# Two transformer layers on one core: a weight tile's last eighth stored apart, one weight load a head sooner, panels that end in turn, splits in a given order

## The chip, the cores and the metric

The kernel runs on one core of one Trainium2 chip. The metric is the device time of one execution in microseconds (us); less is better. Inside a core five engines work side by side, each on its own list of instructions, strictly in the order of that list: TensorE (PE in the profile, with its weight loads as PEld), VectorE (DVE), ScalarE (ACT), GpSimd (POOL) and SyncE (SP). An instruction whose data aren't there yet holds up all that stands behind it on its engine. SP and POOL also issue the DMA transfers that bring weights from device memory.

## The reference

Two consecutive layers work on 512 latent tokens and 256 context tokens of 1024 features, in float32. Each layer normalises and modulates its input, projects it, attends, projects the heads' outputs back to 1024 features (the output projection), adds that to the residual, and runs a gated feed-forward network (FFN).

```python
# layer 0 (even): latent attention heads and neighbourhood heads side by side
p = h @ even_w_in
o = concat(mla_heads(p...), na_heads(p...))        # 8 + 8 heads
x = x + gate * (o @ even_w_out)                    # output projection, 1024 x 1024
x = x + gate * swiglu(modulate(x), w_gate_up, w_down)
# layer 1 (odd): sliding-window grouped-query attention with sinks, latent tokens only
o = swa(h @ odd_w_in)
x = x + gate * (o @ odd_w_out)
x = x + gate * swiglu(modulate(x), w_gate_up, w_down)
return rms_norm(x) * final_norm

def swiglu(h, w_gate_up, w_down):
    g, u = split(h @ w_gate_up)                    # 2 x 2816 features
    return (silu(g) * u) @ w_down
```

## The kernel before, in words

**Layout and precision.** Features lie on the 128 partitions and tokens along the free axis, so an activation of 1024 features is 8 tiles (KT = 8). Every float32 operand is held as two numbers of a shorter type, a high part and a low part. A product of two such operands is three matmuls: high by high, high by low, low by high. In `mm3` (L312) these are L319, L321 and L322; in the FFN's `product` they are L1437 to L1439; in `three`, which the FFN's first panels use, L741 to L743. A raw weight tile `wr` arrives by DMA from SP; ScalarE makes its high part `wh` with a cast, then VectorE the low part `wl` by a subtraction. `load_w` (L299) does this with L308 and L309, `parts` (L1423) with L1424 and L1425.

**Buffers.** `wr`, `wh` and `wl` have three slots each, of 1024 columns. A slot comes free only when the last reader of its old tile is through, so the fourth weight tile of a stretch can't be cast before the first tile's last matmul. `nb` (two slots of 768 columns) holds masks and such.

**Output projection.** `output` (L1302) goes over the 8 blocks m of 128 output features, for each of two streams of tokens. Block m needs one weight tile of 128 x 1024: 8 pieces of 128 columns, one for each of the 8 tiles k of attention output. Its 24 matmuls accumulate over k in one of TensorE's result banks (names starting with ps). Layer 0's stream has 384 tokens, layer 1's 256. The last tiles of attention output come late, since they need the last heads.

**What sets the order.** The program is written with a scheduler that takes the instructions of each engine from a list of ready ones by its own estimate of when they start. So the order on an engine may differ from the text, but is fixed before the program runs. `behind(instruction, mark)` adds an ordering wait behind an earlier instruction. DMA loads of weights are issued on SP in that same way, each as soon as its slot `wr` is free.

**FFN.** Layer 0 has 384-token halves, layer 1 256-token halves. The first gate and up panels (`first_pairs`, L1513) are plain products: the second half of the tokens panel by panel, then the first half with three panels interleaved, k by k, as the loop at L1531 has it. All later panels come as a `Pair` (L1441) with seven products of sums of operands instead of eight (a Strassen-like scheme): `head` two products, `body` three (s2, s3, s1) and `tail` two (s4 for "22", u2 for "T4"). `weights` makes the sums s1 to s4 of the weights on VectorE and splits each into high and low. A chunk of three or four panels (`CHUNKS`, L28; two in layer 0's last) ends with the products of `w_down`. In layer 0's last chunk `keep_groups` loads all of that chunk's `w_down` columns ahead, and the last `output` of layer 0 uses them. `late_step` puts modulation sums of layer 1 (L273, each 128x1024 on VectorE) into FFN stretches.

## Time and profile before

| | |
|---|---|
| time, median of 3 runs | 1554.52 us (1552.96 to 1556.51) |
| the profiled execution's own time | 1556.14 us |
| its span in the profile | 1554.4 us |
| granted clock of TensorE, mean | 0.995 of full speed |
| TensorE busy | 1524.9 us, 98% of the span |
| VectorE, ScalarE, GpSimd busy | 76%, 49%, 13% |
| DMA traffic | 225.95 MB, mean 145 GB/s |

All readings of the trace are of that one profiled execution, which took 1.6 us more than the median; 1.7 us of it lie outside the span. In timeline rows the first two numbers are the start from the span's begin and the length in us, then engine, line, operation, `out<-in`, the shape, and in brackets the idle time before it with the instruction that ended it. Matmuls overlap, so their spacing is read from start to start. Lines are those of the kernel before; the changed kernel's `mm3` has L342, L344 and L345, its residual add L1300, its `parts` L1461 and L1462.

### The profile page before, as it was taken

Reading aid. Unit: us, or ns where it says so; the run is one execution under the profiler, and the core shown is the slowest. Engines: PE = TensorE matmul, PEld = TensorE weight load, DVE = VectorE, ACT = ScalarE, POOL = GpSimd, SP = SyncE. Lnnn points to the kernel's source line nnn. Section 1 sums busy time; section 2 is a strip of 40 time slices with the busy share of each in tenths; the row PEclk is TensorE's granted clock in tenths of the full one; section 3 lists DMA queues with packets and bytes.
Section 4 is the critical chain, followed back from the end, with each engine's and each line's share of the span. In section 5 each row is a group of like instructions: output and inputs, shape, how many; then the busy total and the mean of one; then the engine's idle time right before and its main releaser. Section 6 shows DMA issues by size and latency. Waiting matters only on the chain.

```text
span 1554.4 us, 26610 instructions
## 1 busy us (share of the span) xinstructions
PE 1524.9 (98%) x10032; PEld 1373.6 (88%) x10032; DVE 1182.5 (76%) x2420; ACT 760.7 (49%) x1523; POOL 195.4 (13%) x266
## 2 busy tenths in 40 slices
PE   9999899999999999999999999999999999999998
PEld 8788787878999898999989998877889899898997
DVE  4799987776867686867768667789867779678685
ACT  4533676673555242433424335557846455354453
POOL 0022211000111102012021122560011000000001
PEclk9999999999999999999999999999999999999999
DMA  9675654244643636547375493200224224324322
GB/s 322 245 223 182 161 143 102 57 132 135 216 136 120 232 102 219 174 146 286 117 258 183 165 341 128 68 28 1 96 81 138 82 72 137 105 76 135 89 90 88
DMA packets 80931, 225.95 MB, mean 145 GB/s; under 512 B 11233, under 2 KB 18401, under 8 KB 80801
## 3 DMA queue, kind: packets, MB, share of 16 engines
q1 hardware_dynamic: 61968, 148.73, 30.3%
q0 software_dynamic: 17680, 73.94, 13.8%
q8 instruction: 79, 1.29, 0.3%
q10 hardware_dynamic: 1152, 1.57, 0.3%
q14 instruction: 52, 0.42, 0.1%
HBM read 186.97 MB, written 23.07 MB: 135 GB/s over the span
## 4 chain that ended last, share of the span: by engine, by line
PE 75%; DVE 8%; ACT 2%; issue 2%; DMA 2%; POOL 0%; DVEq 0%; ACTq 0%; POOLq 0%
PE pss L1439 5%; PE pso L530 5%; PE pss L1438 5%; PE pss L1437 5%; PE psd L319 3%; PE psd L321 3%; PE psd L322 3%; PE pss L319 3%; PE pss L322 3%; PE pss L321 3%; PE pst L1439 3%; PE pst L1437 3%; PE pst L1438 3%; PE pst L319 2%; PE pst L321 2%; PE pst L322 2%
## 5 line engine op out<-in xcount | busy, mean ns | idle before, releaser
L308 ACT CAST wh<-wr 128x1024 fp32r<-128x1024 f32 (+2 forms) x147 | 115.1, 798 | 224.1 <-DMA wr<-in_w_dn_dram 44.6
L309 DVE TENSOR_TENSOR wl<-wr,wh 128x1024 fp32r<-128x1024 f32 (+2 forms) x144 | 130.3, 912 | 87.4 <-ACT wh L308 83.2
L537 ACT ACTIVATE p<-p,sm 128x512 f32<-128x512 f32 (+3 forms) x144 | 105.1, 731 | 30.7 <-DVE sm L541 30.1
L1437 PE MATMUL pss<-b,wh 128*128 128x384 f32 (+1 forms) x346 | 107.6, 312 | 0.5 <-ACT b L345 0.5
L1438 PE MATMUL pss<-b,wh 128*128 128x384 f32 (+1 forms) x346 | 107.8, 312 | 0.1
L1439 PE MATMUL pss<-b,wl 128*128 128x384 f32 (+1 forms) x346 | 107.1, 311 | 0.4 <-DVE wl L1425 0.4
L321 PE MATMUL psd<-b,wh 128*128 128x512 f32 (+2 forms) x254 | 88.7, 349 | 0.0
L273 DVE CUSTOM_DVE_ANT_0 p<-rope,cond 128x1024 bf16<-128x1024 f32 x64 | 76.9, 1219 | 12.3 <-DMA rope<-in_mod_w_dram 12.2
L319 PE MATMUL psd<-b,wh 128*128 128x512 f32 (+2 forms) x214 | 78.7, 368 | 0.9 <-ACT wh L308 0.3
L322 PE MATMUL psd<-b,wl 128*128 128x512 f32 (+2 forms) x214 | 77.6, 363 | 0.0
L263 POOL DMA_DIRECT2D rope<-in_mod_w_dram x48 | 25.6, 534 | 411.6 <-DVE mod L273 390.9
L530 PE MATMUL pso<-ph,b 128*64 128x256 f32 (+1 forms) x400 | 77.0, 351 | 0.4 <-DVE ph L475 0.2
L530 PE MATMUL pso<-pl,b 128*64 128x256 f32 (+1 forms) x400 | 77.2, 351 | 0.0
L1439 PE MATMUL pst<-b,wl 128*128 128x384 f32 (+1 forms) x226 | 70.7, 313 | 1.0 <-DVE wl L1425 1.0
L1437 PE MATMUL pst<-b,wh 128*128 128x384 f32 (+1 forms) x226 | 70.6, 313 | 0.6 <-ACT p L1487 0.6
L1438 PE MATMUL pst<-b,wh 128*128 128x384 f32 (+1 forms) x226 | 70.5, 312 | 0.0
L1424 ACT CAST wh<-pl 128x512 fp32r<-128x512 f32 x78 | 45.0, 619 | 51.1 <-PE pss L1438 22.5
L1424 ACT CAST wh<-wr 128x1024 fp32r<-128x1024 f32 x39 | 41.0, 1052 | 56.8 <-PE pst L1438 14.8
L319 PE MATMUL pss<-st,wh 128*128 128x512 f32 (+2 forms) x198 | 67.6, 341 | 0.3 <-ACT wh L308 0.3
L322 PE MATMUL pss<-st,wl 128*128 128x512 f32 (+2 forms) x198 | 67.6, 341 | 0.1
L321 PE MATMUL pss<-b,wh 128*128 128x256 f32 (+2 forms) x208 | 66.0, 317 | 0.0
L1437 PEld LDWEIGHTS pss<-b,wh 128*128 128x128 f32 x346 | 65.0, 188 | 1.1 <-ACT b L345 0.8
(627 smaller groups left out, 5256.8 us busy)
## 6 DMA issues: line engine op xcount, KB each, us to landing
wr<-in_w_gu_dram SPq DMA_DIRECT2D x88, 512.0 KB, 4.0
rope<-in_mod_w_dram POOLq DMA_DIRECT2D x48, 512.0 KB, 3.9
wr<-in_w_dn_dram SPq DMA_DIRECT2D x73, 256.0 KB, 2.8
wr<-in_w_out_dram SPq DMA_DIRECT2D x32, 512.0 KB, 4.0
p<-home POOLq DMA_DIRECT2D x40, 384.0 KB, 5.6
home<-p POOLq DMA_DIRECT2D x40, 384.0 KB, 5.3
wr<-in_w_in_dram SPq DMA_DIRECT2D x21, 512.0 KB, 4.0
ph<-in_mod_w_dram SPq DMA_DIRECT2D x24, 256.0 KB, 3.0
```

The lines of the kernel that those rows point to most:

```text
L273: behind(V.tensor_tensor_reduce(out=T("p", [P, D], mybir.dt.bfloat16), in0=w, in1=cond[:, v, :], op0=ALU.mult, op1=ALU.add, scale=1.0, sca ...
L308: behind(S.copy(h, r), *after[:1])
L309: behind((G if eng else V).tensor_tensor(lo, r, f(h), op=ALU.subtract), *after[1:])
L319: ins = PE.matmul(o, wh[:, k], mh[:, c], start=first and k == 0, stop=False)
L321: PE.matmul(o, wh[:, k], ml[:, c], start=False, stop=False)
L322: PE.matmul(o, wl[:, k], mh[:, c], start=False, stop=last and k == n - 1)
L530: ins = PE.matmul(o[64 * i : 64 * i + 64, c], v(kt), t, start=n == 0, stop=n == len(moving[i]) - 1)
L537: S.activation(p[:, c], p[:, c], AF.Exp, bias=nm, scale=-1.0, accum_out=dn)
L1424: S.copy(h, t)
L1437: PE.matmul(o, wh, xh, start=first and k == 0, stop=False, skip_group_check=not first)
L1438: PE.matmul(o, wh, xl, start=False, stop=False, skip_group_check=not first)
L1439: PE.matmul(o, wl, xh, start=False, stop=k == 3, skip_group_check=not first)
```

## The change

Four things are done.

1. **Ends apart.** For the first three weight tiles of the first stream of both attention output projections, a new `load_ends` takes the place of `load_w`. The raw tile is loaded whole. Its first 896 columns (k = 0 to 6) go to `wh` and `wl` as before, and its last 128 (k = 7) to a piece of a tile `nb`, whose six pieces of 128 columns hold the high and low ends of all three tiles. The class `Ends` picks the right one for k. In layer 0 the first of these tiles is loaded by `mla_jobs` while head 6 of 8 is at work; before, it came after the last head's text.
2. **Panels end in turn.** In layer 1's three interleaved panels, the first four k are interleaved as before, and then each panel's last four k come in one piece, panel after panel.
3. **Splits in order.** In the first pair of each layer 1 chunk, the subtraction that makes s4 and the low part of u2 wait for s2's low part. In layer 0's last pair, and for the first split in `keep_groups`, they wait for the low part of the gate weights.
4. **First products sooner.** At the end of layer 0's FFN, the k = 0 products with the first kept tile (five with its high part) are issued before the last pair's tail; `output` picks up that open bank and goes on from k = 1.

VectorE and ScalarE each have six instructions more, the casts and subtractions of the six ends.

```diff
+    class Ends:
+        def __init__(self, head, end):
+            self.head, self.end, self.n = head, end, head.shape[1] // P
+        def __getitem__(self, at):
+            k = at[1]
+            return self.head[:, k * P : k * P + P] if k < self.n else self.end
+    begun, begun_ends = [], []
+    def load_ends(src, spare, m, after=()):
+        r, n = T("wr", [P, D]), D - P
+        dma(r, src)
+        h, lo = T("wh", [P, n], F32R), T("wl", [P, n], F32R)
+        ends = [spare[:, x * P : x * P + P] for x in (2 * m, 2 * m + 1)]
+        for x, (y, z) in ((r[:, :n], (h, lo)), (r[:, n:], ends)):
+            behind(S.copy(y, x), *after)
+            behind(V.tensor_tensor(z, x, f(y), op=ALU.subtract), *after)
+        return tuple(Ends(x, y) for x, y in zip((h, lo), ends))
...
 # mla_jobs
+            if h == 6:
+                begun_ends.append(T("nb", [P, NT], F32R))
+                begun.append(load_ends(I["w_out0"][0], begun_ends[0], 0))
...
 # output
-                w = kept[m] if keep and i else keep(src, m) if callable(keep) else load_w(src(m), len(mov), P, LOE[l, comp, i], "b" if keep else None, held[m : m + 1] * 2 if i == 0 else ())
+                if comp == 2 and i == 0 and m < 3:
+                    w = begun.pop() if begun else load_ends(src(m), ends(), m, held[m : m + 1])
+                else:
+                    w = kept[m] if keep and i else keep(src, m) if callable(keep) else load_w(src(m), len(mov), P, LOE[l, comp, i], "b" if keep else None)
...
-                o = banks([c], PG)
-                ins = mm3(o, w, mov)
+                n = len(opened)
+                o = opened.pop() if n else banks([c], PG)
+                ins = mm3(o, [x[:, n:] for x in w] if n else w, mov[n:], first=not n)
...
 # Pair.weights
+            self.low = marks["low"]
...
             self.s2 = parts(s2, *(x[:, h[0]] for x in w2))
+            late = {None: (), "g": (self.low,), "s": (marks["low"],)}[self.order]
...
-            V.tensor_tensor(s4, g[:, h[1]], s2, op=ALU.subtract)
+            behind(V.tensor_tensor(s4, g[:, h[1]], s2, op=ALU.subtract), *late)
             self.s4 = parts(s4, *(x[:, h[1]] for x in w3))
-            self.u2 = parts(u[:, h[1]], T("ph", [P, 512], F32R), T("pl", [P, 512], F32R))
+            self.u2 = parts(u[:, h[1]], T("ph", [P, 512], F32R), T("pl", [P, 512], F32R), late)
...
 # first_pairs
-            for x, k in enumerate((0, 4, 1, 5, 2, 6, 3, 7)):
-                for n, o in zip(ns, os):
-                    after = when.pop(len(steps), ())
-                    steps.append(behind(three(o, [y[:, k] for y in ws[n]], ops[a[k // 4]][k % 4], x == 0, x == 7)[0], *after))
+            cut = 4 if l else KT
+            turns = [(x, n, o) for x in range(cut) for n, o in zip(ns, os)]
+            turns += [(x, n, o) for n, o in zip(ns, os) for x in range(cut, KT)]
+            for x, n, o in turns:
+                k, after = (0, 4, 1, 5, 2, 6, 3, 7)[x], when.pop(len(steps), ())
+                steps.append(behind(three(o, [y[:, k] for y in ws[n]], ops[a[k // 4]][k % 4], x == 0, x == 7)[0], *after))
...
 # ffn
-                    p = Pair(l, j, ops, cs, tags[j - k0], (near_done[3],) if j == DIRECT[l] and l == 0 else ())
+                    p = Pair(l, j, ops, cs, tags[j - k0], (near_done[3],) if j == DIRECT[l] and l == 0 else (),
+                             "s" if l and j == k0 else "g" if l == 0 and j == NFF - 1 else None)
...
-            if last:
+            if l == 0 and ci == len(CHUNKS[l]) - 1:
+                o = banks([LATS], PG)
+                first = mm3(o, [x[:, :1] for x in ahead[0]], hs[:1], last=False)
+                opened.append(o)
+                last.tail((first,))
+            elif last:
                 last.tail()
```

How the lists move is seen at three places. The first is TensorE's list at the end of layer 0's attention: `pst` rows are transposes of the last heads' scores (L484 before, L507 after), `pss` rows with 128x384 are the output projection's block 0. Before:

```order
L484 MATMUL pst_4004<-ident_r_90,p_3927 128x128
L484 MATMUL pst_4004<-ident_r_90,p_3958 128x128
L484 MATMUL pst_4011<-ident_r_90,wr_3977 128x128
L484 MATMUL pst_4011<-ident_r_90,p_3987 128x128
L484 MATMUL pst_4011<-ident_r_90,wr_3977 128x128
L484 MATMUL pst_4011<-ident_r_90,p_3987 128x128
L319 MATMUL pss_4252<-b_3502,wh_4248 128x384
L321 MATMUL pss_4252<-b_3503,wh_4248 128x384
L484 MATMUL pst_4032<-ident_r_90,wr_3977 128x128
```

The same place with the change:

```order
L507 MATMUL pst_4013<-ident_r_90,p_3927 128x128
L507 MATMUL pst_4013<-ident_r_90,p_3958 128x128
L342 MATMUL pss_4255<-b_3502,wh_3994 128x384
L344 MATMUL pss_4255<-b_3503,wh_3994 128x384
L345 MATMUL pss_4255<-b_3502,wl_3995 128x384
L342 MATMUL pss_4255<-b_3696,wh_3994 128x384
L344 MATMUL pss_4255<-b_3697,wh_3994 128x384
L345 MATMUL pss_4255<-b_3696,wl_3995 128x384
L342 MATMUL pss_4255<-b_3837,wh_3994 128x384
L344 MATMUL pss_4255<-b_3838,wh_3994 128x384
L345 MATMUL pss_4255<-b_3837,wl_3995 128x384
L507 MATMUL pst_4020<-ident_r_90,wr_3977 128x128
```

Nine products of block 0 now stand ahead of a group of transposes, where two stood behind it.

The second place is TensorE's list where the first three blocks end (`st_4232` and `st_4241` are the high part of attention tile k = 7). Before:

```order
L319 MATMUL pss_4252<-st_4232,wh_4248 128x384
L319 MATMUL psd_4289<-st_4232,wh_4285 128x384
L319 MATMUL pss_4333<-st_4232,wh_4329 128x384
L321 MATMUL pss_4252<-st_4233,wh_4248 128x384
L322 MATMUL pss_4252<-st_4232,wl_4249 128x384
L321 MATMUL psd_4289<-st_4233,wh_4285 128x384
L322 MATMUL psd_4289<-st_4232,wl_4286 128x384
L321 MATMUL pss_4333<-st_4233,wh_4329 128x384
L322 MATMUL pss_4333<-st_4232,wl_4330 128x384
L319 MATMUL pst_4369<-b_3502,wh_4365 128x384
L321 MATMUL pst_4369<-b_3503,wh_4365 128x384
L319 MATMUL pss_4411<-b_3502,wh_4407 128x384
```

With the change:

```order
L345 MATMUL pst_4376<-b_3502,wl_4373 128x384
L342 MATMUL pst_4376<-b_3696,wh_4372 128x384
L344 MATMUL pst_4376<-b_3697,wh_4372 128x384
L345 MATMUL pst_4376<-b_3696,wl_4373 128x384
L342 MATMUL pst_4376<-b_3837,wh_4372 128x384
L342 MATMUL pss_4255<-st_4241,nb_3991 128x384
L342 MATMUL psd_4294<-st_4241,nb_3991 128x384
L342 MATMUL pss_4340<-st_4241,nb_3991 128x384
L344 MATMUL pst_4376<-b_3838,wh_4372 128x384
L344 MATMUL pss_4255<-st_4242,nb_3991 128x384
L345 MATMUL pss_4255<-st_4241,nb_3991 128x384
L344 MATMUL psd_4294<-st_4242,nb_3991 128x384
```

The k = 7 products of blocks 0 to 2 read the ends in `nb`, and products of the next two blocks stand ahead of them.

The third place is VectorE's list in the first pair of a layer 1 chunk. Before (L1467 makes s4; the L1425 row with `pl_13387` is u2's low part, `wl_13365<-ph_13371` is s2's):

```order
L1460 TENSOR_TENSOR ph_13371<-pl_13370,wr_13358 128x512
L1463 TENSOR_TENSOR ph_13376<-wr_13358,wr_13359 128x512
L1274 SCALAR_TENSOR_TENSOR b_12112<-pst_13339,mod_1832_8983,b_12112 128x512
L1467 TENSOR_TENSOR pl_13382<-wr_13358,ph_13371 128x512
L1425 TENSOR_TENSOR pl_13387<-wr_13359,ph_13386 128x512
L1425 TENSOR_TENSOR wl_13365<-ph_13371,wh_13364 128x512
```

With the change:

```order
L1498 TENSOR_TENSOR ph_13385<-pl_13384,wr_13372 128x512
L1502 TENSOR_TENSOR ph_13390<-wr_13372,wr_13373 128x512
L1300 SCALAR_TENSOR_TENSOR b_12119<-pst_13353,mod_1833_8990,b_12119 128x512
L1462 TENSOR_TENSOR wl_13379<-ph_13385,wh_13378 128x512
L1506 TENSOR_TENSOR pl_13396<-wr_13372,ph_13385 128x512
L1462 TENSOR_TENSOR pl_13401<-wr_13373,ph_13400 128x512
```

s2's low part now stands ahead of s4 and of u2's low part. Between the two attention output projections, in layer 1's sliding-window attention, no line of the program is changed, yet the scheduler puts a few of TensorE's instructions there in another order: the two lists differ at 17 places.

More of the change, by code (lines that the diff above doesn't have):

```diff
@@ L1287, in kept_w, with keep_groups @@
         return ahead[m]
-    def keep_groups(k0, kc):
+    def keep_groups(k0, kc, low):
         n = NT // (kc * P)
@@ L1297, in keep_groups @@
                 I["w_dn"][0, a:z, :, k0 * P : (k0 + kc) * P].rearrange("m p c -> p m c"))
-            parts(r[:, c], *(x[:, c] for x in t))
+            parts(r[:, c], *(x[:, c] for x in t), (low,) * (a == 0))
             for m in range(a, z):
@@ L1304, in output, with ends @@
         rest, kept, done = iter(()), [], []
+        spare = []
+        def ends():
+            if not spare:
+                spare.append(begun_ends.pop() if begun_ends else T("nb", [P, NT], F32R))
+            return spare[0]
         for i, (c, v) in enumerate(streams):
@@ L1341, in hybrid_kernel @@
     home = [dr.tile([P, NT], F32, name=f"home{k}") for k in range(KT)]
-    near_done, near_cast = [], []
+    near_done, near_cast, opened = [], [], []
     def combined(src, l, comp, c1, c2):
@@ L1429, in hybrid_kernel, with product @@
     output(lambda m: I["w_out0"][m], O, 0, 2, ((TOK2, 0), (TOK1, 0)), norm, LATE[0])
-    def product(o, w, x, first=False):
+    def product(o, w, x, first=False, after=()):
         for k in range(4):
@@ L1436, in product @@
             xh, xl = x[k]
-            PE.matmul(o, wh, xh, start=first and k == 0, stop=False, skip_group_check=not first)
+            behind(PE.matmul(o, wh, xh, start=first and k == 0, stop=False, skip_group_check=not first), *after)
             PE.matmul(o, wh, xl, start=False, stop=False, skip_group_check=not first)
@@ L1441, in hybrid_kernel, with __init__ @@
     class Pair:
-        def __init__(self, l, j, ops, cs, tag, after=()):
-            self.after = after
+        def __init__(self, l, j, ops, cs, tag, after=(), order=None):
+            self.after, self.order = after, order
             self.l, self.j, self.ops, self.c1, self.c2 = l, j, ops, *cs
@@ L1488, in body, with tail @@
             self.done = marks["middle"] = V.tensor_tensor(self.t[:, self.c2], self.y, self.t[:, self.c2], op=ALU.add)
-        def tail(self):
-            product(self.z, self.s4, self.ops["22"])
+        def tail(self, after=()):
+            product(self.z, self.s4, self.ops["22"], after=after)
             marks["silu"] = S.activation(self.s[:, self.c2], self.z, AF.Silu)
@@ L1557, in ffn @@
                     if l == 0 and j == NFF - 1:
-                        keep_groups(k0, kc)
+                        keep_groups(k0, kc, p.low)
                     p.body()
```

## The prediction

> **What bounds the kernel now.** I read the page's busy rows and chain first, then busy time by stretch, then the engines' timelines at the places where the order moves.
>
> ```profile
> PE 1524.9 (98%) x10032; PEld 1373.6 (88%) x10032; DVE 1182.5 (76%) x2420; ACT 760.7 (49%) x1523; POOL 195.4 (13%) x266
> PE 75%; DVE 8%; ACT 2%; issue 2%; DMA 2%; POOL 0%; DVEq 0%; ACTq 0%; POOLq 0%
> 340.00:384.00 44.00, 40.61 (x260) 32.99 (x257) 27.17 (x52) 21.82 (x42) 0.53 (x1) 1.00 0.45 154
> 1060.00:1140.00 80.00, 78.60 (x641) 62.60 (x639) 71.33 (x237) 63.00 (x152) 0.00 (x0) 1.00 0.14 47
> 1355.00:1362.00 7.00, 6.58 (x57) 6.38 (x56) 7.00 (x12) 3.53 (x8) 0.00 (x0) 1.00 0.45 150
> ```
>
> (The last three rows: stretch, its length, then busy time of PE, PEld, DVE, ACT and POOL, granted clock, DMA share and GB/s.) TensorE bounds the kernel: 98% busy, three quarters of the chain. No matmul is removed here, so the only thing to win is its idle time, 1554.4 - 1524.9 = 29.5 us in all, of which 44.00 - 40.61 = 3.4 us lie in the 44 us where layer 0's attention passes into its output projection. Busy time hides more: matmuls restarting after a wait overlap less, so I count from start to start.
>
> **Ends apart, layer 0.** PE first, then ACT and SP's queue.
>
> ```profile
> 346.71 0.27 PE L484 MATMUL pst<-ident_r,p 128*128 128x128 f32 x1
> 348.22 0.44 PE L319 MATMUL pss<-b,wh 128*128 128x384 f32 x1 [1.24 <-ACT wh L308]
> 349.29 0.27 PE L484 MATMUL psd<-ident_r,wr 128*128 128x128 f32 x1
> 350.07 0.33 PE L484 MATMUL psd<-ident_r,p 128*128 128x128 f32 x1 [0.50 <-ACT p L537]
> 364.78 0.27 PE L484 MATMUL pst<-ident_r,p 128*128 128x128 f32 x1
> 365.40 0.33 PE L484 MATMUL pst<-ident_r,wr 128*128 128x128 f32 x1 [0.35 <-DVE pl L475]
> 374.80 0.34 PE L321 MATMUL pss<-st,wh 128*128 128x384 f32 x1
> 374.98 0.34 PE L322 MATMUL pss<-st,wl 128*128 128x384 f32 x1
> 375.58 0.45 PE L319 MATMUL pst<-b,wh 128*128 128x384 f32 x1 [0.26 <-ACT wh L308]
> 377.48 0.44 PE L319 MATMUL psd<-b,wh 128*128 128x384 f32 x1 [0.34 <-ACT wh L308]
> ...
> 346.21 0.40 ACT L1226 CAST st<-b 128x256 fp32r<-128x256 f32 x1
> 347.12 1.05 ACT L308 CAST wh<-wr 128x1024 fp32r<-128x1024 f32 x1
> 348.06 0.94 ACT L537 ACTIVATE wr<-wr,sm 128x768 f32<-128x768 f32 x1
> 374.48 2.95 ACT L308 CAST wh<-wr 128x1024 fp32r<-128x1024 f32 x3 [2.28 <-PE pss L321]
> ...
> 337.06 3.95 SPq L134 DMA_DIRECT2D b<-in_xn_dram  x8
> ```
>
> A 128x384 product starts 0.18 us after the one before (374.80 to 374.98); a 128x256 product, by its columns, 0.12, a 128x512 product 0.24. The transposes follow each other in about 0.1.
>
> The first tile's cast stands at 347.12, so the first product waits to 348.22: 1.51 - 0.11 = 1.40 us lost. Loaded one head sooner, the tile is cast in an earlier gap (on SP the second tile's load goes out ahead of the eight residual loads of 337.06, which nothing reads before block 0 is summed), and nine products (1.6 us of work) stand where the wait was. The same cast pushed the exponentials (348.06), for which the transpose at 350.07 waits: 0.78 - 0.11 = 0.67. With the cast out of the way I strike that too, and the later one at 365.40, a copy behind a delayed softmax: 0.62 - 0.11 = 0.51. Then the casts of tiles 3 to 5, three in a row from 374.48, start only when the last k = 7 product of tile 0 has let go of a slot. From 374.98 to 377.48 five starts should take 0.88 us and take 2.50: 1.62 lost. With the ends in `nb` the slots are free after k = 6, and other products stand ahead of k = 7. Gone in all: 1.40 + 0.67 + 0.51 + 1.62 = 4.20. Not all stays gone: going through the new lists instruction by instruction with these durations, I find one wait left near 362, where two copies on VectorE stand behind the subtractions of tiles 2 and 3, worth about 0.55. Taken: **3.65**, between 1.0 (only the first wait goes, in part) and 4.2.
>
> The wait is moved onto others: on ScalarE the copies of the scores stand behind the casts of tiles 1 and 2, whose DMAs are issued on SP once a raw slot is free. If a tile lands late, its cast holds those copies, and TensorE waits for them. By the replay tile 2 has about 1 us to spare.
>
> **The split itself.** It adds six casts and six subtractions. The nearest casts are 0.40 for 256 columns and 1.05 for 1024, a line of 0.00085 us a column on a start of 0.18. So 896 + 128 columns cost 0.94 + 0.29, 0.18 more than whole; six tiles 1.1 us of ScalarE, in stretches where ACT is busy 21.82 of 44 us, and as much again on DVE at 27.17. If all lay on the path it would cost 1.1; beside the matmuls nothing. Taken: **-0.3**, as about two of the six fall among the copies TensorE waits for.
>
> [...]
>
> **Ends apart, layer 1.** PE, then ACT:
>
> ```profile
> 1150.10 0.28 PE L322 MATMUL pst<-st,wl 128*128 128x256 f32 x1
> 1151.63 0.39 PE L319 MATMUL psd<-st,wh 128*128 128x256 f32 x1 [0.44 <-ACT wh L308]
> 1152.15 0.38 PE L322 MATMUL pss<-st,wl 128*128 128x256 f32 x1
> ...
> 1149.58 2.94 ACT L308 CAST wh<-wr 128x1024 fp32r<-128x1024 f32 x3 [4.44 <-PE psd L321]
> ```
>
> The three casts begin at 1149.58 after 4.44 us of idle for a product, and TensorE eats them as they come. Five starts from 1150.10 to 1152.15 take 2.05 and should take 0.60: 1.45 lost. By my replay the k = 0 to 6 products of tile 0 end some 2 us before 1149.58, more than the loss. Taken **1.3** (0.6 to 1.45).
>
> **Panels in turn.**
>
> ```profile
> 1208.42 0.28 PE L743 MATMUL pst<-b,wl 128*128 128x256 f32 x1
> 1209.02 0.38 PE L741 MATMUL pss<-ph,wh 128*128 128x256 f32 x1 [0.32 <-ACT wh L308]
> 1210.23 0.39 PE L741 MATMUL pst<-ph,wh 128*128 128x256 f32 x1 [0.48 <-ACT wh L308]
> ...
> 1207.92 1.05 ACT L308 CAST wh<-wr 128x1024 fp32r<-128x1024 f32 x1 [1.56 <-PE psd L742]
> ```
>
> Five starts from 1208.42 to 1210.23 take 1.81 for 0.60: 1.2 lost to two casts that wait until the interleaved panels free their slots. In the new list panel 0's last reading of its high part comes three products sooner, not a whole panel, so the casts move by 3 x 0.12. Taken: **0.35** (0 to 1.2).
>
> **Splits in order.** PE of three layer 1 chunks and of layer 0's end, then DVE there:
>
> ```profile
> 1247.17 0.28 PE L1438 MATMUL pss<-st,wh 128*128 128x256 f32 x1
> 1247.97 0.39 PE L1439 MATMUL pss<-st,wl 128*128 128x256 f32 x1 [0.52 <-DVE wl L1425]
> 1295.71 0.39 PE L1439 MATMUL pss<-st,wl 128*128 128x256 f32 x1 [0.36 <-DVE wl L1425]
> 1361.17 0.39 PE L1439 MATMUL pss<-b,wl 128*128 128x256 f32 x1 [0.42 <-DVE wl L1425]
> 918.47 0.34 PE L1439 MATMUL pss<-b,wl 128*128 128x384 f32 x1
> 919.77 0.45 PE L1439 MATMUL pst<-b,wl 128*128 128x384 f32 x1 [0.95 <-DVE wl L1425]
> ...
> 915.88 0.68 DVE L1425 TENSOR_TENSOR pl<-wr,ph 128x512 fp32r<-128x512 f32 x1
> 916.48 0.94 DVE L1425 TENSOR_TENSOR nb<-wr,nb 128x768 fp32r<-128x768 f32 x1
> 918.50 1.22 DVE L1425 TENSOR_TENSOR wl<-wr,wh 128x1024 fp32r<-128x1024 f32 x1
> ```
>
> At 1247.97 the wait is 0.80 - 0.12 = 0.68, at 1295.71, idle 0.36 against 0.52, about 0.5; there s2's low part stands behind s4 and u2's, both needed later. It now comes 1.2 us sooner and both go: **1.2** (0.5 to 1.2). The wait at 1361.17 is another: it is the next pair's gate weights that are late, on a VectorE busy 7.00 of 7.00, and the list is the same; nothing there. At 919.77 the wait is 1.30 - 0.18 = 1.12. u2's low part (915.88) and the kept weights' (916.48) step behind the gate's low part, which comes at least 917.42 - 915.88 = 1.5 sooner: **1.1** (0.5 to 1.12). The products of s4, u2 and the kept tiles are several products later; by the replay none of them becomes the wait.
>
> **First products sooner.**
>
> ```profile
> 935.82 0.34 PE L1439 MATMUL pst<-b,wl 128*128 128x384 f32 x1
> 936.78 0.44 PE L1437 MATMUL pst<-b,wh 128*128 128x384 f32 x1 [0.62 <-ACT p L1487]
> ```
>
> The wait is 0.96 - 0.18 = 0.78, for a copy out of the bank that the tail writes next. Five 128x512 products, 1.2 us, now stand in it. But the tail's end, and with it the last panel's splits that the k = 1 products need, moves back by what the five take beyond the wait, 1.2 - 0.8 = 0.4. Taken: **0.45** (0 to 0.8).
>
> **What is moved without being meant.** The sliding-window attention is listed otherwise at 17 places; nothing in the trace tells the sign. With VectorE busy 71.33 of 80 us a moved piece can expose a wait, or cover one; PE's own idle there is 80.00 - 78.60 = 1.4. I take **-0.5** (-3 to +1.4).
>
> Sum: 3.65 - 0.3 + 1.3 + 0.35 + 1.2 + 1.1 + 0.45 - 0.5 = 7.25 us. The profiled execution, 1556.14, becomes 1548.9; it lies 1.6 above the median of the runs, so against 1554.52 I forecast **1547.3 us**. All upper ends together would give 11.0 less.
>
> **Rivals.**
>
> *The waits come back at the next weight.* If the second or third tile's cast stands ahead of the copies and its transfer lands over 1 us late, layer 0's 3.65 shrinks to about 0. For it: ScalarE and VectorE run in order, and the loads wait for raw slots. Against: half of ScalarE's time is free there. Time: 1547.3 + 3.65 = 1551.0.
>
> *The change doesn't do what it says at the small places.* The two casts at 1209.02 and 1210.23 stay, as panel 0 ends only three products sooner; the pairs' wait goes over to another split on the same VectorE; the five products wait for their own input. Then 0.35, 1.2, 1.1 and 0.45 all fall away: 1547.3 + 3.1 = 1550.4. For it: at 1361.17 the next low part is late although no s4 precedes it. Against: 1.1 at 919.77 has its margin in quoted rows.
>
> *The sliding-window attention pays: slower.*
>
> ```profile
> ACT p L537 <- DVE sm L541: 7.0, 12, 1.3
> ```
>
> (Waits between 1060 and 1140: total us, times, longest.) There ScalarE already waits 12 times for VectorE's maxima, up to 1.3 us. If each of the 17 places sets a 128x512 operation of VectorE (0.68) ahead of what TensorE waits for, that costs 11.6 instead of my 0.5: 1547.3 + 11.1 = 1558.4. It decides from 7.75 / 0.68, some 12 places, on. Against: TensorE's own idle is 1.4 us in 80, with buffers of scores between the engines that take such shifts up.
>
> **How the numbers follow.** Forecast 0.66; waits come back 0.16; small places fail 0.12; attention pays 0.06. 0.2% is 3.1 us, about what a measurement of this kernel can tell from no change: 1551.4 and 1557.6. The forecast case and most of the second and third lie below 1551.4: 0.66 x 0.97 + 0.28 x 0.5 = **0.78** faster; 0.16 within, **0.06** slower. Range: upward both middle rivals (1551.0) and some of their sum, to 1552.5; downward half of what the upper ends add, to 1543.5.
>
> **What would show it.** In the changed profile: the first 128x384 products about a microsecond sooner, with no ACT wait ahead; the six ends cast at 0.29 each; the casts of tiles 3 to 5 ahead of the first products of k = 7, no wait in front of the three following blocks; in layer 1 the cast triple about 2 us sooner; no L1462 wait in the places of 1247.97, 1295.71 and 919.77, but still one at 1361.17; 17 places of the attention with the same 80 us. I am wrong if layer 0's stretch still has a cast or copy wait over 1 us, or if a stretch without a changed line is longer by more than a microsecond.

## The result, and the profile after

The changed kernel takes 1543.86 us, median of 5 runs (1543.17 to 1545.68), beside 1553.35 for the kernel before (5 runs, 1552.24 to 1556.51). The ratio is 0.9934 (95% interval 0.9922 to 0.9947). Timed a second time beside before it gave 0.9946 (0.9932 to 0.9959). The forecast was 1547.3, a gain of 7.25 us, with a range from 1543.5 on; the medians show a gain of 9.5, and the time lies 0.4 above the lower end of that range. The direction and the places were right, the size was too small.

The page of the changed kernel, busy time and chain:

```profile
PE 1522.3 (99%) x10032; PEld 1374.2 (89%) x10032; DVE 1181.0 (77%) x2426; ACT 762.0 (49%) x1529; POOL 194.7 (13%) x266
PE 79%; DVE 6%; ACT 2%; issue 1%; DMA 1%; POOL 0%; DVEq 0%; ACTq 0%; SPq 0%; POOLq 0%
```

TensorE has as many matmuls as before and is busy nearly as long; its idle time fell from 29.5 to 1542.1 - 1522.3 = 19.8 us. Where layer 0's attention ends, the stretch of the changed kernel (columns as in the prediction) has no idle left at all:

```profile
340.00:380.00 40.00, 40.00 (x265) 35.75 (x263) 28.95 (x55) 20.67 (x40) 1.07 (x2) 1.00 0.55 185
```

Since both kernels issue 10032 matmuls and the order differs only locally, the two traces can be laid side by side by the number of the matmul. The time from one number to another then is the price of a stage, whatever happened earlier. Between the two profiled executions (1554.4 and 1542.1 us of span) the 12.3 us come from these places:

| matmuls (time in before) | before | after | gain |
|---|---|---|---|
| 0 to 1100 (to 184 us), no edit | 183.03 | 179.36 | 3.67 |
| 2280 to 2650 (336 to 398), end of layer 0's attention | 61.94 | 56.45 | 5.49 |
| 5600 to 5950 (909 to 976), last pair of layer 0 | 67.22 | 66.27 | 0.95 |
| 6200 to 6820 (1027 to 1108), attention of layer 1 | 80.36 | 81.87 | -1.51 |
| 6820 to 7094 (1108 to 1142), the same, its end | 34.10 | 33.62 | 0.48 |
| 7094 to 7200 (1142 to 1156), layer 1's output projection | 14.24 | 12.68 | 1.56 |
| 7600 to 7700 (near 1209), panels in turn | 13.13 | 12.64 | 0.49 |
| 7840 to 9100 (1240 to 1426), pairs | 183.80 | 182.68 | 1.12 |

Two rows have no edit behind them: 3.67 at the front, and a loss of 1.51 in the sliding-window attention. The experiments deal with both.

At the end of layer 0's attention, TensorE of the changed kernel, then ScalarE and VectorE:

```profile
342.25 0.60 PE L507 MATMUL pst<-ident_r,p 128*128 128x128 f32 x4
342.60 0.42 PE L342 MATMUL pss<-b,wh 128*128 128x384 f32 x1
368.13 0.34 PE L345 MATMUL pst<-b,wl 128*128 128x384 f32 x1
368.30 0.34 PE L342 MATMUL pst<-b,wh 128*128 128x384 f32 x1
368.48 0.34 PE L342 MATMUL pss<-st,nb 128*128 128x384 f32 x1
...
343.44 0.94 ACT L331 CAST wh<-wr 128x896 fp32r<-128x896 f32 x1
344.29 0.29 ACT L331 CAST nb<-wr 128x128 fp32r<-128x128 f32 x1
333.77 1.08 DVE L332 TENSOR_TENSOR wl<-wr,wh 128x896 fp32r<-128x896 f32 x1
334.77 0.28 DVE L332 TENSOR_TENSOR nb<-wr,nb 128x128 fp32r<-128x128 f32 x1
```

The first product starts right behind the transposes, where before 1.51 us passed. Around 368 products follow at 0.17 with no wait for a cast, and the k = 7 products read `nb`. The pieces cost what the two rows of before gave: 0.94 and 0.29.

The other places, TensorE of the changed kernel (layer 1's output projection with its casts, the panels, the first and second chunk's pair, layer 0's last pair):

```profile
1141.00 0.28 PE L345 MATMUL pst<-st,nb 128*128 128x256 f32 x1
1141.12 0.29 PE L342 MATMUL pss<-st,wh 128*128 128x256 f32 x1
1141.36 0.28 PE L342 MATMUL psd<-st,wh 128*128 128x256 f32 x1
1138.35 3.08 ACT L308 CAST wh<-wr 128x1024 fp32r<-128x1024 f32 x3 [2.33 <-PE psd L344]
...
1197.75 0.28 PE L766 MATMUL pst<-b,wl 128*128 128x256 f32 x1
1197.87 0.39 PE L764 MATMUL pss<-ph,wh 128*128 128x256 f32 x1
1199.08 0.39 PE L764 MATMUL pst<-ph,wh 128*128 128x256 f32 x1 [0.47 <-ACT wh L308]
...
1235.77 0.39 PE L1474 MATMUL pst<-st,wh 128*128 128x256 f32 x1 [0.27 <-ACT wh L1461]
1236.38 0.28 PE L1476 MATMUL pss<-st,wl 128*128 128x256 f32 x1
1238.27 0.38 PE L1476 MATMUL pst<-st,wl 128*128 128x256 f32 x1
1283.86 0.28 PE L1476 MATMUL pss<-st,wl 128*128 128x256 f32 x1
909.39 0.34 PE L1476 MATMUL pss<-b,wl 128*128 128x384 f32 x1
909.56 0.34 PE L1476 MATMUL pst<-b,wl 128*128 128x384 f32 x1
925.62 0.34 PE L1476 MATMUL pst<-b,wl 128*128 128x384 f32 x1
925.98 0.50 PE L342 MATMUL pst<-st,nb 128*128 128x512 f32 x1
935.73 0.50 PE L342 MATMUL pst<-st,nb 128*128 128x512 f32 x1 [0.18 <-ACT st L1461]
```

In layer 1 the cast triple now starts 2.8 us ahead of its first product (1138.35 against 1141.12) and no product waits. Of the panels' two waits the first is gone, the second stays (1199.08). In the first chunk's pair the wait for s2's low part is gone (1236.38), but about 0.2 each comes up on either side (1235.77, and 1238.27, which starts 0.36 after the product before it). The wait for the gate's low part in layer 0 is gone (909.39 to 909.56). The five early products start 0.36 after the product before them, and where `output` takes their bank up again there is a new wait (935.73).

### The profile page after: what moved, and what is told of

It is laid out like the page before. It is cut to its first block, busy times and chain, and to the rows that moved or that the text cites. A ratio compares the mean times of both kernels' runs of the same rounds, so it can differ in the third digit from the quotient of the medians.

```text
span 1542.1 us, 26615 instructions
## 1 busy us (share of the span) xinstructions
PE 1522.3 (99%) x10032; PEld 1374.2 (89%) x10032; DVE 1181.0 (77%) x2426; ACT 762.0 (49%) x1529; POOL 194.7 (13%) x266
## 3 DMA queue, kind: packets, MB, share of 16 engines
q10 hardware_dynamic: 1152, 1.57, 0.3%
## 4 chain that ended last, share of the span: by engine, by line
PE 79%; DVE 6%; ACT 2%; issue 1%; DMA 1%; POOL 0%; DVEq 0%; ACTq 0%; SPq 0%; POOLq 0%
PE pso L553 5%; PE pss L1476 5%; PE pss L1475 5%; PE pss L1474 5%; PE psd L342 4%; PE psd L344 3%; PE psd L345 3%; PE pss L342 3%; PE pss L345 3%; PE pss L344 3%; PE pst L1476 3%; PE pst L1474 3%; PE pst L1475 3%; PE pst L342 3%; PE pst L507 3%; PE pst L344 3%
## 5 line engine op out<-in xcount | busy, mean ns | idle before, releaser
L308 ACT CAST wh<-wr 128x512 fp32r<-128x512 f32 (+2 forms) x141 | 109.2, 788 | 217.5 <-DMA wr<-in_w_dn_dram 47.2
L309 DVE TENSOR_TENSOR wl<-wr,wh 128x512 fp32r<-128x512 f32 (+2 forms) x138 | 123.3, 900 | 90.3 <-ACT wh L308 85.9
L273 DVE CUSTOM_DVE_ANT_0 p<-rope,cond 128x1024 bf16<-128x1024 f32 x64 | 76.9, 1221 | 12.3 <-DMA rope<-in_mod_w_dram 12.0
L345 PE MATMUL pss<-st,wl 128*128 128x256 f32 (+2 forms) x195 | 66.6, 341 | 0.1
L344 PE MATMUL pss<-b,wh 128*128 128x256 f32 (+2 forms) x207 | 66.3, 320 | 0.0
L1474 PEld LDWEIGHTS pss<-b,wh 128*128 128x128 f32 x346 | 65.0, 188 | 1.0 <-ACT b L368 0.8
L1475 PEld LDWEIGHTS pss<-b,wh 128*128 128x128 f32 x346 | 65.0, 188 | 0.9 <-DVE b L369 0.6
```

Of the source, the lines that this page charges most:

```text
L273: behind(V.tensor_tensor_reduce(out=T("p", [P, D], mybir.dt.bfloat16), in0=w, in1=cond[:, v, :], op0=ALU.mult, op1=ALU.add, scale=1.0, sca ...
L308: behind(S.copy(h, r), *after[:1])
L309: behind((G if eng else V).tensor_tensor(lo, r, f(h), op=ALU.subtract), *after[1:])
L344: PE.matmul(o, wh[:, k], ml[:, c], start=False, stop=False)
L345: PE.matmul(o, wl[:, k], mh[:, c], start=False, stop=last and k == n - 1)
L1474: behind(PE.matmul(o, wh, xh, start=first and k == 0, stop=False, skip_group_check=not first), *after)
```

## The experiments

Stages below are given as in the table, by the number of the matmul.

**The kernel before, once more; layer 0's ends alone; everything but these; layer 1's ends alone.** The theory after the result: each edit's gain is its own and lies at its place; the ends in layer 0 bring 5.4; the 3.7 at the front is chance. The rival was that a side effect brings the 3.7 each time: with `nb` used for the ends, GpSimd issues two loads into `nb` later (the expectations call them mask loads; they bring modulation weights).

The last three kernels differ from the changed one by

```diff
 # layer 0's ends alone: the edits 2, 3 and 4 undone, and
-                if comp == 2 and i == 0 and m < 3:
+                if l == 0 and comp == 2 and i == 0 and m < 3:
 # all but layer 0's ends: no load at h == 6, and
+                if l == 1 and comp == 2 and i == 0 and m < 3:
 # layer 1's ends alone: the same, and the edits 2, 3 and 4 undone
```

> The kernel before, unchanged, profiled once more. Theory: the 3.7 us by which the changed kernel was ahead at 190 us is chance of one execution, since TensorE's, VectorE's and ScalarE's lists are the same up to 330 us; then this profile reaches the 1100th matmul (184.1 us in the first profile, 180.5 in the changed one) anywhere between those two. Rival: two mask loads of GpSimd that the use of nb moves later make the difference each time; then it reaches it again at 184.1 us, within 0.3. Time 1553.4 either way, ratio 1.000.

> The ends apart and the earlier load in layer 0 alone. Theory: the stretch from 335 to 385 us gains 5.4 us, as in the changed kernel's profile, more than the 3.35 of the prediction, and nothing else moves: 1553.4 - 5.4 = 1548.0. Rival (the mask loads on GpSimd, which move with this edit alone): the first 190 us gain 3.7 more, each time: 1544.3, and the 1100th matmul starts at 180.5 us within 0.3.

> The changed kernel without the ends apart and the earlier load in layer 0; all else kept. Theory: the other edits gain what their places show, 1.0 at 919, 0 at 936, 0.6 in the sliding-window attention, 1.6 at 1150, 0.5 at 1209, 1.1 in the pairs: 4.8 in all, 1548.6. The prediction's own terms make it 1.3 + 0.35 + 1.2 + 1.1 + 0.45 - 0.5 = 3.9, 1549.5. Rival (mask loads): the first 190 us are as slow as before, 184.1 us at the 1100th matmul within 0.3; by chance it may be anything between 180.5 and 184.1.

> The ends apart in layer 1's output projection alone. Its list differs from before's in the sliding-window attention too. Theory: 1.6 us gone from 1141 to 1155, and the reordered attention from 1040 to 1140 gains 0.6 of itself: 1553.4 - 2.1 = 1551.3. Rival: the attention's 0.6 was chance (or lies in another edit); then only 1.6, and 1551.8, or the prediction's allowance of 0.5 lost, 1552.3. Read from the stretches, since the times hardly tell these apart.

Measured:

| | time, us | ratio (95%) | 0 to 1100 | 2280 to 2650 | 6820 to 7094 | 7094 to 7200 |
|---|---|---|---|---|---|---|
| before once more | 1553.36 | 1.0001 (0.9993 to 1.0010) | 180.40 | 62.00 | 34.09 | 14.24 |
| layer 0's ends alone | 1546.68 | 0.9957 (0.9945 to 0.9970) | 182.02 | 56.45 | 34.09 | 14.24 |
| all but layer 0's ends | 1549.79 | 0.9973 (0.9964 to 0.9982) | 181.49 | 61.95 | 33.62 | 12.68 |
| layer 1's ends alone | 1552.27 | 0.9986 (0.9976 to 0.9996) | 180.85 | 61.98 | 33.63 | 12.68 |

The front was chance: the kernel before, unchanged, did its first 1100 matmuls 2.6 us sooner the second time, and layer 0's ends, which move these loads, left it between the two. In the trace of before these loads also start only at 224.6 and 227.2 us, behind the front. That rival falls. Layer 0's ends, with the earlier load, bring 5.5 us in every kernel that has them and in none that hasn't. Layer 1's ends bring 1.56 in the projection, and 0.47 in the attention ahead of it in both kernels that have them. The parts' ratios, 0.9957 and 0.9973, are 6.7 and 4.2 us; the sum, 10.9, fits the whole (10.3 by its ratio, between 8.2 and 12.1) within the intervals.

**The halves of layer 0's edit, the split by itself, the early products by themselves.** Is it the earlier load or the ends that brings 5.5, and what does it cost to cut a cast in two?

```diff
 # earlier load alone, on the kernel before
+            if h == 6:
+                begun.append(load_w(I["w_out0"][0], KT, P))
...
+                w = begun.pop() if begun else kept[m] if ...
 # ends without the earlier load: the changed kernel less
-            if h == 6:
-                begun_ends.append(T("nb", [P, NT], F32R))
-                begun.append(load_ends(I["w_out0"][0], begun_ends[0], 0))
 # split alone, on the kernel before, for the same tiles of both layers
+        r, h, lo = T("wr", [P, D]), T("wh", [P, D], F32R), T("wl", [P, D], F32R)
+        for c in (slice(0, D - P), slice(D - P, D)):
+            behind(S.copy(h[:, c], r[:, c]), *after)
+            behind(V.tensor_tensor(lo[:, c], r[:, c], f(h[:, c]), op=ALU.subtract), *after)
 # early products alone: edit 4, with edits 1, 2 and 3 undone
```

> The kernel before with one thing done: layer 0's first output tile is loaded, whole, at head 6; no end is stored apart. Theory: the waits at the front of the stretch go (1.40, 0.67, 0.38, 0.51, 0.14 and 0.29 with 0.33 of slow restarts, 3.7 in all), and the three casts that wait for tile 0's last k = 7 product stay with 1.4 and 0.3 of restarts: the 370 matmuls from about 336 to 398 us take 58.2 to 58.5 instead of 61.95. Rival: the early load alone moves the waits on to the next tiles, and the ends are what brings the 5.5; then 60 or more.

> The changed kernel without the earlier load: ends apart in both layers, the first tile of layer 0 loaded where it was. Theory: the three casts' 1.7 goes and the front's 3.7 mostly stays, as the first cast stands where it stood: the same 370 matmuls take 60.0 to 60.5 (56.45 with both, 61.95 with neither), the sum of the two halves being additive within 0.5. Rival: the ends free the casts in the whole stretch, so that most of the gain comes without the early load: under 58.5.

> The kernel before, with the first three tiles of both attention output projections cast and subtracted in two pieces of 896 and 128 columns into the same whole tile: nothing is freed earlier, only the instructions are split. It measures the price of the split by itself. Theory: nothing measurable in layer 0, 61.95 +- 0.2 for the 370 matmuls, since no wait ends on the small pieces; the cast of 128 columns takes 0.29. The prediction took 0.3 for both layers, the fixed cost in full would be 0.55 in each. The lists of the sliding-window attention move here as they do in the changed kernel: if its gain of 0.57 from 1040 to 1140 us comes from that order, it is here too; if it comes from the freed tiles, it is not.

> The five k = 0 products ahead of the last pair's tail, alone. Theory: the wait of 0.79 at 936 shrinks to about 0.2 to 0.4 and another of 0.3 comes up some ten microseconds later, where the k = 1 products wait for the last cast; the 250 matmuls from 925 to 965 us, 48.76 before, stay within 0.3 of it. The prediction's term is 0.45 gained: 48.3. Rival: it costs, 49.3 or more.

Measured, one profile each (time 1548.7, 1547.1, 1551.3 and 1551.5 us, beside one run of before at 1556.7):

| | 2280 to 2650 | of it 2350 to 2528 | of it 2528 to 2540 | 6820 to 7094 | 7094 to 7200 | 5600 to 5950 |
|---|---|---|---|---|---|---|
| before | 61.94 | 29.32 | 3.88 | 34.10 | 14.24 | 67.22 |
| earlier load alone | 58.20 | 25.59 | 3.88 | 34.10 | 14.25 | 66.63 |
| ends, load not earlier | 60.63 | 29.81 | 2.10 | 33.63 | 12.67 | 66.38 |
| split alone | 60.89 | 28.27 | 3.89 | 33.63 | 14.24 | 67.08 |
| early products alone | 61.96 | | | 34.10 | 14.25 | 68.38 |
| all | 56.45 | 25.63 | 2.11 | 33.62 | 12.68 | 66.27 |

The two gains add up, each at its place: the earlier load takes 3.7 out of the front of the stretch, the ends take 1.8 out of the twelve matmuls where the three casts were waited for, together 5.5. Without the earlier load the ends' kernel has a wait that neither before nor the changed kernel has, TensorE first, then ScalarE and VectorE:

```profile
360.92 0.27 PE L507 MATMUL pst<-ident_r,p 128*128 128x128 f32 x1
362.92 0.63 PE L374 MATMUL pst<-ident_r,pl 128*128 128x128 f32 x4 [1.73 <-DVE ph L498]
359.87 1.05 ACT L308 CAST wh<-wr 128x1024 fp32r<-128x1024 f32 x1 [1.73 <-DMA wr<-in_w_out_dram]
360.95 1.22 DVE L309 TENSOR_TENSOR wl<-wr,wh 128x1024 fp32r<-128x1024 f32 x1 [2.22 <-ACT wh L308]
362.09 1.28 DVE L498 COPY ph<-pst 128x512 f32<-128x512 f32 x2
```

Two copies of VectorE stand behind the subtraction of a weight tile, the fourth, that waits for its cast, and the cast waits for the tile's transfer. This is the wait that the prediction had put "near 362" and kept in the sum. It is real, and worth 1.9 here (2.00 from start to start, where 0.1 is the pace), but it is there only if the first tile is late, and with it those behind it. In the changed kernel the fourth tile is cast 4.4 us earlier, and the subtraction and the copies behind it hold nothing up:

```profile
355.47 1.05 ACT L308 CAST wh<-wr 128x1024 fp32r<-128x1024 f32 x1
356.62 1.22 DVE L309 TENSOR_TENSOR wl<-wr,wh 128x1024 fp32r<-128x1024 f32 x1
358.02 1.29 DVE L498 COPY ph<-pst 128x512 f32<-128x512 f32 x2 [0.18 <-PE pst L507]
```

The split alone was expected to change nothing in layer 0 (61.95 +- 0.2). It gained 1.05. Between the two pieces of the first cast the exponential comes through, TensorE and ScalarE of that kernel:

```profile
345.15 0.44 PE L328 MATMUL pss<-b,wh 128*128 128x384 f32 x1 [1.13 <-ACT wh L317]
344.15 0.94 ACT L317 CAST wh<-wr 128x896 fp32r<-128x896 f32 x1
344.99 0.94 ACT L546 ACTIVATE wr<-wr,sm 128x768 f32<-128x768 f32 x1
345.92 0.28 ACT L317 CAST wh<-wr 128x128 fp32r<-128x128 f32 x1
```

That is the smaller part: by matmul 2400, past these rows, only 0.16 is gained. The other 0.9 comes between 2420 and 2480, where TensorE's list of this kernel has another order, and the waits of before at 359.51 (0.38) and 365.40 (0.51) do not occur. What in that order brings it was not singled out. So in this stretch the split cost nothing, against the 0.3 that was set aside for it; most of the 1.05 goes with the order that came with it. And the 0.47 in the sliding-window attention is here too, though no slot comes free earlier: six more instructions in the next stage shift the order of the attention, as the lists show, and that order runs 0.47 faster. Which of the 17 places brings it was not singled out. Layer 1's 1.56 is not here: that needs the ends.

The early products alone don't gain but lose: the first of them waits 1.20 for the cast that makes its input, where the wait they should fill was 0.79. The 250 matmuls of the expectation (5700 to 5950) take 49.17, beside 48.77 before: between the theory and the rival. Not all of the microsecond in the table's last column is theirs, since the first 100 matmuls of it lie ahead of them, and these take from 18.5 to 19.3 in kernels without any edit there (18.45 before, 19.21 here).

**The remaining edits.** Layer 0's ordered splits alone, and panels in turn with layer 1's ordered splits (edit 1 undone in both layers, edit 4 undone in both kernels).

> The ordered splits of layer 0's last pair and of the first kept group, alone. So far the wait at the gate's low part (1.12 in the first profile, 1.5 to 1.7 in five others without this edit) is gone in every kernel that has it, but they all have the early k = 0 products too, which alone made the wait at 936 longer (1.20 for 0.79). Theory: the 350 matmuls from about 906 to 965 us take 67.1 without either edit (mean of six profiles), 68.4 with the early products alone; here 65.7 +- 0.5, and the wait of 0.79 at 936 is as before, so that the early products bring nothing on top (66.7 mean with both). Rival: the splits put off for it come late at 936, a wait over 1.2 there, and 66.7 or more.

> Panels that end in turn and layer 1's ordered splits, alone; their places lie apart. Theory: at 1209 the 100 matmuls take 12.65 (13.1 without), 0.45 gained; of the pairs the first chunk's place takes 8.6 (9.1 without, mean of seven) and the second's 31.3 (31.8), 1.0 in all; the third and fourth chunk are as scattered as they are without it (23.9 to 24.6 and 16.1 to 17.1). The prediction's terms: 0.35 and 1.2. Rival: part of what these places gained in the changed kernel came from the other edits; then less than 0.2 at either.

Layer 0's splits alone (1554.1 us, before 1554.2; a dip of TensorE's granted clock, 0.72 on the mean from 350 to 355 us, cost this execution 1.55 elsewhere, 63.50 from 2280 to 2650): 66.14 from 5600 to 5950, within the 65.7 +- 0.5. Its profile has no such dip near 955, of which more below; two profiles of kernels without the edit that lack it too took 66.46 and 66.63, so the gain there is 0.4. Where the dip is present, five kernels without either edit took 67.1 to 68.3, four with both 66.3 to 67.4; a fifth with both and without the dip took 65.42. But the second half of that theory fell. The wait at 936 is not as before: with these splits in order, the scheduler puts the five products ahead of the tail by itself, and the first of them waits 1.38:

```profile
934.93 0.34 PE L1473 MATMUL pst<-b,wl 128*128 128x384 f32 x1
936.48 0.50 PE L342 MATMUL pst<-st,nb 128*128 128x512 f32 x1 [1.21 <-ACT st L1458]
```

Accordingly the lists of TensorE, VectorE and ScalarE of the changed kernel are the same with edit 4 and without it: in this kernel the fourth edit does nothing. Cut in two, the stage shows two effects of opposite sign. From 5600 to 5700, at the wait for the gate's low part, the six profiles with the ordered splits take 17.2 to 17.6 and the eight without them 18.5 to 19.3: 1.6 gained. From 5700 to 5800 the seven profiles with the products ahead of the tail take 20.2 to 21.3 and the seven without 19.98 to 20.04: about 0.55 lost. So the early products, which the ordered splits bring along, cost a third of what these gain.

Panels and layer 1's splits (1554.2 us by its single time, which can't show a gain this small): 12.65 against 13.1 at the panels, as expected, 0.45. At the first chunk 8.42 against a mean of 9.06 without the edit, 0.6; at the second 31.50 against a mean of 31.76, where 31.3 had been expected. The third and fourth chunk are as scattered as without it.

By place, means over all profiles with and without each edit give:

| edit and place | forecast | measured |
|---|---|---|
| layer 0, earlier load and ends (with the split's 0.3) | 3.35 | 5.5 |
| layer 1, ends | 1.3 | 1.56 |
| sliding-window attention, order | -0.5 | 0.47, and 0.1 before it |
| panels in turn | 0.35 | 0.46 |
| layer 1, ordered splits, four chunks together | 1.2 | 0.8 |
| layer 0, ordered splits and early products | 1.55 | 0.9 |
| sum | 7.25 | 9.8 |

The dip of the clock in the sliding-window attention, 1.6 us in both profiles of the changed kernel, is not in this sum; with it the sum is 8.2. The medians show 9.5, and the ratio's interval reaches from 8.2 to 12.1, so the times don't tell whether the dip is there in most executions.

**The front of the kernel, and a version that might be faster still.** What makes 3 us of difference between executions of one program in its first 190 us? Each profile has TensorE's wait near 170 either at 4.4 or at about 0.9 twice, and beside it a sum on VectorE that takes 2.2 for 0.17. GpSimd is subtracting at those moments. The second kernel here gives these three subtractions to VectorE:

```diff
-                    wu[x] = load_w(I["w_" + x], 2, m, G, queue=G)
+                    wu[x] = load_w(I["w_" + x], 2, m, queue=G)
```

> The changed kernel, unchanged, beside the next run on the same chip. Theory: 0.6 to 0.7% under before, about 1544. Its profile may show the wait near 170 us either at 0.9 or at 4.4, as the ten profiles so far do in six and four cases, whatever the kernel.

> The changed kernel with GpSimd's three subtractions near 158 and 168 us (the low parts of three small weight tiles) given to VectorE. In every profile VectorE's modulation sums beside them take 2.9 and 1.8 us for 0.75 and 0.69, and in four of ten a sum of 8 columns takes 2.2 for 0.17, and TensorE then waits 4.4 us instead of 0.9 and 0.9. Theory: VectorE is held up while GpSimd subtracts; without that, no such wait, the spread of the times shrinks from some 4 us to 2, and the median falls by 1 to 3 us against the changed kernel: 1542. Rival: the three subtractions cost VectorE 3.7 us where it is the busiest engine, and the new order of the neighbourhood heads brings other waits; no gain, or slower than the changed kernel.

Measured: the changed kernel again 1545.10 (1544.14 to 1547.19), the other 1543.93 (1541.64 to 1545.68), ratios to before 0.9946 (0.9932 to 0.9959) and 0.9934 (0.9921 to 0.9948). The intervals overlap; whether it is faster isn't settled, and its spread, 4.0 us, isn't smaller. The rows show what the move does to VectorE, though. The changed kernel in its second profile, TensorE, GpSimd, VectorE, and TensorE's clock in two stretches:

```profile
170.70 0.58 PE L754 MATMUL pss<-st,st 128*128 128x256 f32 x1 [4.23 <-DVE sm L564]
157.25 4.10 POOL L309 TENSOR_TENSOR wl<-wr,wh 128x1024 fp32r<-128x1024 f32 x2 [9.20 <-ACT wh L308]
166.57 2.84 POOL L309 TENSOR_TENSOR wl<-wr,wh 128x1024 fp32r<-128x1024 f32 x1 [5.23 <-ACT wh L308]
157.31 2.88 DVE L237 CUSTOM_DVE_ANT_0 p<-pl,cond,mod 128x512 bf16<-128x512 f32 x1
160.13 1.77 DVE L237 CUSTOM_DVE_ANT_0 p<-ph,cond 128x512 bf16<-128x512 f32 x1
167.26 2.18 DVE L241 SCALAR_TENSOR_TENSOR mod<-mod,modb 128x8 f32<-128x8 f32 x1
...
165.00:170.00 5.00, 1.47 (x13) 1.27 (x11) 4.89 (x9) 2.61 (x3) 2.84 (x1) 0.85 0.76 211
170.00:175.00 5.00, 4.30 (x20) 4.30 (x21) 4.12 (x16) 4.32 (x14) 0.58 (x1) 0.50 0.45 109
```

And VectorE with GpSimd's subtractions gone:

```profile
157.24 0.75 DVE L237 CUSTOM_DVE_ANT_0 p<-pl,cond,mod 128x512 bf16<-128x512 f32 x1
157.92 0.69 DVE L237 CUSTOM_DVE_ANT_0 p<-ph,cond 128x512 bf16<-128x512 f32 x1
161.45 1.22 DVE L309 TENSOR_TENSOR wl<-wr,wh 128x1024 fp32r<-128x1024 f32 x1
```

In the first, the VectorE sums that start inside a GpSimd subtraction end with it or little later: 161.90 for 161.35, 169.44 for 169.41. In the second the same sums take 0.75 and 0.69, and its profile has no 4.4 us wait. The three subtractions cost VectorE 1.22, 0.69 and 1.22.

## Why the prediction was right or wrong

The bound was right: TensorE's idle time was all there was to win, and nearly all of it was won at the places that were named. The time was forecast 3.4 us too high. Of this 1.2 is no step of the prediction but the median of before, 1554.52 in the forecast and 1553.35 beside the changed kernel. The other 2.2 are gain, and the step that failed is the term for layer 0's stretch: 3.65, less 0.3 for the split, where 5.5 was measured, above the term's own upper end of 4.2. The places were right there, and the size was not. Two other errors, 1.0 too low in the sliding-window attention and 1.05 too high in the ordered splits and early products taken together, cancel by luck.

- **What was struck.** The prediction struck 1.40 + 0.67 + 0.51 + 1.62 = 4.20. The trace of before holds three more waits there, 0.38 (358.96 to 359.51), 0.14 and 0.29 (two near 366), and a slow restart of 0.1 behind a wait, 0.3 in all at the front and 0.1 more at the casts. With them the stretch holds about 5.4 of waits and restarts; the changed kernel removes 5.49. The earlier load alone removes 3.74, as these front terms add up to (3.7), and the ends remove 1.8 at the casts (1.62).
- **What was kept back.** 0.55 for a wait near 362, which the earlier load makes away with, and 0.3 for the split, which cost nothing: 0.85 in all. Reading the new order with fixed durations found a wait that is real in the kernel without the earlier load, where the fourth tile's cast starts at 359.87; in the changed kernel that tile is cast at 355.47, and the wait is gone.
- **The split's fixed cost.** The pieces took 0.94 and 0.29 as worked out, 0.18 more than whole. None of it shows as a loss: the kernel with the split alone even gained 1.05 in layer 0, by another order of TensorE's list.
- **The sliding-window attention** was put at -0.5 (-3 to +1.4) and gained 0.47 by its order, without a reason that was singled out. The price of 11.6 of the slower rival is excluded: the attention's two stages together take 113.9 with the new order and 114.5 with the old one, where no dip of the clock falls into them. This is the second term that was off, by 1.0.
- **Layer 1's ends** (1.3 for 1.56) **and the panels** (0.35 for 0.46) were right, with the second cast's wait left as forecast.
- **Layer 1's ordered splits** gained 0.8 instead of 1.2: both named waits go, but neighbours of 0.2 take their place in the first chunk. The wait at 1361.17, said to stay, is not there in the changed profile (that product starts 0.11 after the one before it); it comes and goes with and without the edit (that chunk's stage lies between 23.9 and 24.6 without it, 23.9 and 24.2 with it), so neither the forecast nor its absence says anything of the edit.
- **Layer 0's splits and the early products** gained 0.9 instead of 1.1 + 0.45. The splits gained 1.6, since the wait that they remove is 1.2 to 1.7 in the other seven profiles without them and was 1.12 in the one that was read; the early products lose about 0.55. The rival "doesn't do what it says" was right for these alone: the five products wait for their own input.
- **"The waits come back at the next weight"** did not come true: no cast or copy wait over 0.2 is left in layer 0's stretch.
- **The range.** Its lower end does not follow from its words: half of what the upper ends add would be 1547.3 - 1.9 = 1545.4; 1543.5 is all of it, 1554.52 - 11.0. By its words the range would not have held 1543.86.
- What was forecast of the changed profile held: the ends cast at 0.29, no wait ahead of the first products, the triple in layer 1 ahead of its use. "A stretch without a changed line longer by more than a microsecond" did appear, 1.51 in the sliding-window attention of the changed profile: eight pairs of matmuls at half clock, as the granted clock there shows, seen in the second profile of the same kernel too (81.90), but not in five other kernels with the same attention lists, 80.24 to 80.32. Whether the whole change makes this dip likelier, or two executions had it by chance, stays open.

```profile
1027.00:1031.00 4.00, 4.00 (x24) 2.39 (x23) 3.28 (x11) 1.62 (x4) 0.00 (x0) 0.57 0.00 0
```

## What to carry to other kernels

When an edit removes waits from a stretch of a bound engine, add up all that the stretch loses, small waits and slow restarts too, against its undisturbed pace, and hold back a leftover only after replaying the list with the new arrival times; the few large gaps are not the whole. A large slot that was held by its last eighth was worth splitting here: the ends took 1.8 us out of layer 0's stretch and 1.56 out of layer 1's, the extra cast cost 0.18 us beside other work, and nothing on the path. Before a difference of some microseconds between two profiles is explained, profile the same kernel twice: here 3.7 of 12.3 us were of that kind, and two profiles of one kernel lay 2.6 apart in the same place. An edit that orders one wait away can also move work elsewhere in the list: layer 0's splits brought the early products with them, and gave a third of their gain back.

## What the runs showed of the hardware

- **VectorE's sums took longer beside a GpSimd subtraction.** In the changed kernel's second profile, two sums of 128x512 and one of 128x8 that started inside a GpSimd subtraction took 2.88, 1.77 and 2.18 us; with the three subtractions given to VectorE, the same sums took 0.75, 0.69 and 0.17. By what the one engine holds up the other, no run shows.
- **Half clock for one or two steps of 3.41 us, in some executions.** TensorE's granted clock falls to one half at a handful of places: 0.50 in the 5 us behind the 4.4 us wait, 0.57 near 1029. In each of the fourteen traces all changes of the clock lie on a grid of 3.41 us, and each dip ahead of the last 30 us is one or two steps long. One dip cost 1.55 us near 350 and 1.57 near 1029. At most places it comes in one execution and not in the next: near 955 in ten of fourteen profiles, near 350 in one. Near 1029 waits of 0.34 and 0.83 lie in the step ahead of it. Near 955 no wait does, but 24 matmuls of one column, which count as busy time; before, and then its clock in the next step:

```profile
955.76 2.73 PE L371 MATMUL psd<-ones,p 128*128 128x1 f32 x24
958.54:961.95 3.41, 3.41 (x17) 3.41 (x17) 1.15 (x3) 1.50 (x3) 2.19 (x3) 0.50 0.99 370
```

  In nine of the ten profiles with this dip, 22 or more of the 24 lie in the one step ahead of it, in the tenth 17; in the four without it no step holds more than 19. So in these profiles the dip goes, with one exception, with how many of the 24 fall into one step of the grid; no run here moves the grid, and what makes the clock fall is not shown.
- **The two are linked at the front.** All profiles with a dip of the clock at 150 to 160 us (0.71 to 0.95) have the short waits at 170 (about 0.9, twice), all those without it the 4.4 us wait, but for the kernel whose subtractions were moved. That the dip shifts the sum out of GpSimd's subtraction fits the rows; no run forces it, so it stays an argument.
